# Cutting the last 272 tokens into 144 and 128, with the sums of squares taken inside the last product

## The chip, the cores and the metric

The kernel runs on one core of a Trainium2 chip. The metric is the device time of one execution in microseconds (us), as the median of three runs. The profile is of one execution, and its lines name the core's engines: PE is TensorE (matmuls), PEld its weight loads, DVE is VectorE, ACT is ScalarE, POOL is GpSimd, and SP is the engine whose queue issues the transfers (DMA) to and from memory. Each engine works through its own instructions in the order in which the program wrote them.

## The reference

One layer of a hybrid convolutional decoder on 1024 prompt tokens and 8 x 8 sample tokens, all float32, model width 1024. The part that the change touches is the end: the feed-forward network's down projection, added to x, and the final norm.

```python
h2 = rmsnorm(x, g_ffn)
f = silu(h2 @ w_gate) * (h2 @ w_up)          # width 2816
x = x + f @ w_down
y = rmsnorm(x, g_final)                      # x * rsqrt(mean(x * x) + EPS) * g_final
```

The norm needs, for each token, the sum of the squares of all 1024 channels, so it can start only when every channel of that token has its last addition.

## The kernel before

The tokens lie along the free dimension and the channels along the 128 partitions: `xt` holds x as 8 blocks of 128 channels by T = 1088 tokens. The tokens are two halves of HT = 544, and each half two pieces of CW = 272. Products are made in float16 with both operands split into a high and a low part, so each 128 x 128 weight tile takes three matmuls (high-high, high-low, low-high; `products`, L250, issued at L266).

The down projection runs in four groups of the feed-forward width. The last group (`last_group`, L1636) has four weight tiles per block of channels, so a block of one piece is 12 matmuls. It does the second half of the tokens first, then the first half: block 0 for the whole half, and then, as the list LAST says (L68), blocks 1 to 7 of the first piece (tokens 0 to 271) and blocks 1 to 7 of the last piece (tokens 272 to 543). Each of these is a task (`last_task`, L1578), and the tasks are emitted in this order. A product goes to one of four accumulators in PSUM, used in turn.

After a block's product, VectorE adds it to x (L1554), ScalarE squares the result (L1568), and the square goes into a running sum per half, `squares[hf]`. That addition is GpSimd's (L1575) for the early blocks and VectorE's for one late block (L341, with EPS); the squares of the last one or two blocks are kept apart in `parts` (LAST_PE: one block for an earlier piece, two for the last). An addition of squares is put in the list of late work and emitted at the start of the next task.

The sum over the 128 partitions is a matmul with a matrix of ones, in float32 (`column_sums`, L284; L291 and L297): one such matmul for the running sum and one for each kept square. A float32 matmul is two passes in the profile. For a piece that isn't the last, the sums are put into a later product: `midway` holds pairs of a fraction and a function, and `products` calls the function when that fraction of its matmuls is emitted. SUMS_AT gives 0.8 for a piece of 272, and the call falls into block 3 of the piece that follows. TensorE takes the sums in its own order, so it waits there if a square is not ready. The sums' accumulator is one of two banks called stat.

The final norm (`final_norm`, L1596) then makes 1/sqrt by one activation (L323) and a Newton step of three VectorE instructions (L326 to L328), scales the eight blocks of x (L1626) and writes y (L1629, SP). For a piece that isn't the last this is a stream of steps: one scaling after each later task, so that in the tasks of the last piece VectorE does one addition and one scaling in turn; what is left is emitted after the last task. For the last piece (`fast`) ScalarE and GpSimd do blocks 2 and 5 (L1617, L332, L333, L1624), VectorE the other six, and y is written in four transfers instead of two.

Of the kernel before, what the change touches and what calls it, by code (L numbers as in the profile page):

```python
# [13 lines left out]
D = 1024  # L14
KB = D // P
# [14 lines left out]
HT = T // 2  # L30
CW = 272
# [33 lines left out]


SEVENTHS = "E1 E2 E3 M1 M2 M3 S21 S22 S23 S31 S32 S33 A1 A2 A3"
LAST = [(0, 272), (272, 272)]  # L68


LAST_PE, LAST_POOL = (1, 2), (2, 5)

SUMS_AT = {HT: 0.6, CW: 0.8}

PAIR = [(0, 0), (0, 1), (1, 0), (1, 1)]
TRIPLE = [(0, 0), (0, 1), (1, 0), (1, 1), (2, 0), (2, 1)]
# [65 lines left out]
def trunk(ctx, tc, x, par, sta, stb, w_in, w_o, w_gu, w_ds, w_dl, y, st_out):  # L142
    nc = tc.nc
    pe, act, dve, gps = nc.tensor, nc.scalar, nc.vector, nc.gpsimd
# [15 lines left out]
    def nm(s):  # L160
        cnt[0] += 1
        return f"{s}{cnt[0]}"
# [8 lines left out]
    def small():  # L171
        return sm.tile([P, HT], F32, tag="s", name=nm("s"))
# [10 lines left out]
    def begin(name, turns):  # L183

        cut_banks(part_b, "b", "ps_" + name)
        psum["phase"], psum["turns"], psum["n"] = name, turns, 0
# [6 lines left out]
    def bank2():  # L193
        k = psum["turns"][psum["n"] % len(psum["turns"])]
        psum["n"] += 1
        return psum[k].tile(
            [P, 2, 512], F32, tag="two", name=nm("two"), bufs=psum["turns"].count(k)
        )

    def single():  # L200
        n = 4 if psum["phase"] == "seven" else 2
        return psum["b"].tile([P, 1, 512], F32, tag="one", name=nm("one"), bufs=n)
# [4 lines left out]
    def stat_banks(wide=False):  # L207
        if psum["phase"] == "tail" and wide:
            return bank2()
        if psum["phase"] == "tail":  # L210
            return psum["b"].tile([P, 1, 512], F32, tag="stat", name=nm("stat"), bufs=2)
        if psum["phase"] == "first":
            return psum["b"].tile([P, 1, 512], F32, tag="stat", name=nm("stat"), bufs=2)
        return psum["b"].tile([P, 2, 512], F32, tag="stat", name=nm("stat"))

    def prm(i):
        return par_t[:, i : i + 1]
# [30 lines left out]
    midway = []  # L248

    def products(outs, terms, first=True, last=True, part=(0, None), low_last=None):  # L250


        todo = [(i, q) for i in range(len(terms)) for q in range(3)]
        if low_last:
            todo.sort(key=lambda a: a[1] == low_last)
        one, end = todo[0], todo[-1]
        todo = todo[slice(*part)]
        for n, (i, q) in enumerate(todo):
            for part_, fn in list(midway):
                if n >= int(part_ * len(todo)):  # L260
                    midway.remove((part_, fn))
                    fn()
            w_, col, acts = terms[i]
            wpart, apart = ((0, 0), (0, 1), (1, 0))[q]
            for out, (hl, t0) in zip(outs, acts):
                pe.matmul(  # L266
                    out,
                    w_[:, wpart, col : col + P],
                    hl[:, apart, t0 : t0 + out.shape[1]],
                    start=first and (i, q) == one,  # L270
                    stop=last and (i, q) == end,
                    skip_group_check=not (first and last),
                )
# [26 lines left out]
    def like(ap, t):  # L300

        return t[:, : ap.shape[1]] if len(ap.shape) == 2 else halves(t[:, : 2 * ap.shape[2]])
# [16 lines left out]
    def rstd_kept(sums, inv_n, scale, copied=False):  # L319

        y0 = like(sums, small())
        t = like(sums, small()) if copied else sums
        act.activation(y0, sums, AF.Abs_reciprocal_sqrt, scale=inv_n)  # L323

        def newton():
            dve.scalar_tensor_tensor(t, sums, -0.5 * scale * inv_n, y0, ALU.mult, ALU.mult)  # L326
            dve.tensor_tensor(t, t, y0, ALU.mult)
            dve.scalar_tensor_tensor(sums, t, 1.5 * scale, y0, ALU.add, ALU.mult)  # L328
            if not copied:
                return sums  # L330
            r = like(sums, small())
            act.activation(r, t, AF.Identity, bias=three_halves[:, 0:1])  # L332
            gps.tensor_tensor(r, r, y0, ALU.mult)  # L333
            return sums, r

        return newton
# [11 lines left out]
    ones = cst.tile([P, P], F32, name="ones")  # L348
# [97 lines left out]
    scaled, loaded, sums = set(), {}, {}  # L446
# [60 lines left out]
    def add(ws, emit, post, *bg):  # L507
        tasks.append((ws, emit, post, bg))
# [322 lines left out]
    keep = {}  # L831
# [621 lines left out]
    def last_products(acc, b, t0, cw, ks=None, **kw):  # L1453
        n0, n1 = GROUPS[LASTG]
        w = whl[W_DN[LASTG, f"D{b}"]]
        n = min(cw, CW)
        outs = [acc[:, i, :n] for i in range(cw // n)]
        hf, o = divmod(t0, HT)
        terms = [
            (w, ((k - n0) // 2 + (k - n0) % 2 * 2) * P, [(fl[k, hf], o + i * n) for i in range(cw // n)])  # L1460
            for k in ks or range(n0, n1)
        ]
        products(outs, terms, **kw)
# [80 lines left out]
    def shaped(ap):  # L1544
        return halves(ap) if ap.shape[1] == HT else ap

    def last_post(b, t0, cw):


        def post(acc):  # L1550
            cols = slice(t0, t0 + cw)
            o = shaped(xt[:, b, cols])
            a = acc[:, :, :CW] if cw == HT else acc[:, 0, :cw]
            dve.scalar_tensor_tensor(o, a, IN_SC, o, ALU.mult, ALU.add)  # L1554
            return last_square(b, t0, cw)

        return post

    def last_square(b, t0, cw):
# [8 lines left out]
        act.activation(sq, xt[:, b, cols], AF.Square)  # L1568
        n_pe = LAST_PE[t0 == LAST[-1][0]]
        if b >= KB - n_pe:  # L1570
# [7 lines left out]
    def last_task(b, t0, cw, *bg):  # L1578
        def emit():
            if (b, t0, cw) == (NWIDE - 1, 0, HT):  # L1580
                begin("tail", "aa")
            if (b, t0) == (NWIDE, LAST[0][0]):
                psum["n"] = 2
            if cw == HT or psum["n"] % 4 < 2:
                acc = bank2()
            else:
                acc = single()
                psum["n"] += 1
            last_products(acc, b, t0, cw)
            return acc  # L1590

        add([W_DN[LASTG, f"D{b}"]], emit, last_post(b, t0, cw), *bg)

    squares, parts = {}, {}

    def final_norm(t0, cw, fast):  # L1596

        hf = t0 // HT
        cols = slice(t0, t0 + cw)
        got = []  # L1600

        def sums():
            c = squares[hf][:, t0 - hf * HT : t0 - hf * HT + cw]
            st = column_sums([shaped(p) for p in [c] + parts.pop(t0, [])])
            got.append(rstd_steps(st, 1.0 / D, 1.0) if cw == HT else rstd_kept(st, 1.0 / D, 1.0, fast))

        if fast:
            sums()
        else:
            if cw < HT:  # L1610
                yield
            midway.append((SUMS_AT[cw], sums))
            while not got:
                yield
        if fast:
            for k in LAST_POOL:
                act.activation(xt[:, k, cols], xt[:, k, cols], AF.Copy, scale=prm(PG3 + k))  # L1617
        r = got[0]()
        if fast:
            r, rs = r  # L1620
        for k in range(KB):
            o = shaped(xt[:, k, cols])
            if fast and k in LAST_POOL:
                gps.tensor_tensor(o, o, rs, ALU.mult)  # L1624
            else:
                dve.scalar_tensor_tensor(o, o, prm(PG3 + k), r, ALU.mult, ALU.mult)  # L1626
            n = 2 if fast else 4
            if k % n == n - 1:
                nc.sync.dma_start(  # L1629
                    y[k + 1 - n : k + 1, :, cols].rearrange("k p t -> p k t"),  # L1630
                    xt[:, k + 1 - n : k + 1, cols],
                )
            if k % 2 == 1 or not fast:
                yield

    def last_group():  # L1636
# [23 lines left out]
        for step in SEVENTHS.split():  # L1660
            last_stage(step[:-1], int(step[-1]))
        norms = [Stream(final_norm(HT, HT, False))]
        for b in range(NWIDE):
            last_task(b, 0, HT, lambda: norms[0](1))
        for t0, cw in LAST:
            for b in range(NWIDE, KB):

                def bg(b=b, t0=t0, cw=cw):
                    for st in norms:
                        st(1)  # L1670
                    if b == KB - 1:
                        norms.append(Stream(final_norm(t0, cw, t0 == LAST[-1][0])))
                        if t0 == LAST[-1][0]:
                            for st in norms:
                                st(100)

                last_task(b, t0, cw, bg)
# [93 lines left out]
```

## Time and profile before

| what | us |
|---|---|
| median of three runs | 1006.96 |
| runs | 1006.45, 1006.96, 1006.99 |
| span of the profiled execution | 1006.2 |
| the profiled execution's own time | not given; the page has its span alone |
| VectorE's addition of the last block (L1554) starts | 995.75 |
| first scaling of the last piece (L1626) starts | 999.39 |

Times in the lines are from the start of the span. A line of a timeline has the start, the length, the engine, the line of the program, the operation, what it writes and reads, the shape and the number of instructions that are merged in it; in brackets stands how long the engine was idle before it, and whose result ended that. A line of a group has the number, then the busy time in us, the mean length of one in ns, and the idle time before them. Instructions of one engine overlap a little: the next one starts some 0.08 us before the one ahead of it has ended, unless it needs its result.

### The profile page before, as it was taken

How to read it: one execution, taken by the hardware profiler on the slowest of the kernel's cores; microseconds unless marked ns; L12 is line 12 of the kernel's file. 1: busy time of each engine (PE TensorE's matmuls, PEld its weight loads, DVE VectorE, ACT ScalarE, POOL GpSimd, SP SyncE). 2: the span in 40 equal slices, each digit the busy share in tenths (PEclk: the TensorE clock that was granted, in tenths of full speed). 3: DMA queues.
4: the chain of work that ended last, by engine and by line, in shares of the span. 5: the costliest groups of instructions: out<-in, count | busy, mean ns of one | idle time of the engine just before them, and what ended most of it. 6: DMA issues, size and time to landing. Idle time of an engine off the chain costs nothing.

```text
span 1006.2 us, 19709 instructions
## 1 busy us (share of the span) xinstructions
PE 982.9 (98%) x8466; PEld 828.0 (82%) x8466; DVE 766.0 (76%) x1095; ACT 398.0 (40%) x713; POOL 380.3 (38%) x310
## 2 busy tenths in 40 slices
PE   5999999999999999999999999999999999999996
PEld 4888888888888888888888888888888888888885
DVE  7949999996676778986775767777676678686667
ACT  6612243247362534543322434322243433234433
POOL 3487895656000206222234223223422322273053
PEclk9999999999999999999999999999999999999998
DMA  9020202111500111120112112011211111131104
GB/s 342 40 84 2 67 26 90 43 43 54 208 2 1 43 43 43 43 74 33 64 43 84 43 43 74 33 64 45 83 43 47 70 33 64 64 127 43 42 2 178
DMA packets 17464, 64.60 MB, mean 64 GB/s; under 512 B 1216, under 2 KB 8528, under 8 KB 12512
## 3 DMA queue, kind: packets, MB, share of 16 engines
q1 hardware_dynamic: 17328, 63.25, 18.0%
q8 instruction: 66, 1.08, 0.4%
q14 instruction: 22, 0.18, 0.1%
q0 software_dynamic: 48, 0.09, 0.0%
HBM read 58.28 MB, written 5.05 MB: 63 GB/s over the span
## 4 chain that ended last, share of the span: by engine, by line
PE 72%; DVE 22%; issue 2%; ACT 2%; POOL 0%; DMA 0%; DVEq 0%; ACTq 0%; POOLq 0%
PE two L266 67%; DVE cv L628 11%; PE one L266 4%; DVE u L282 1%; DVE whl L243 1%; DVE xt L1626 1%; DVE h L282 1%; PE stat L291 1%; DVE v L1116 1%; DVE cv L623 1%; DVE xt L1554 0%; DMA xt<-x 0%; DVE u L606 0%; DVE s L770 0%; DVE s L935 0%
## 5 line engine op out<-in xcount | busy, mean ns | idle before, releaser
L266 PEld LDWEIGHTS <-whl 128*128 128x128 f16 x7374 | 721.0, 98 | 136.5 <-issue 2.7
L266 PE MATMUL two<-u,whl 128*128 128x272 f16 x4416 | 523.0, 279 | 0.9 <-DVE s L1324 0.7
L499 POOL TENSOR_TENSOR s<-wf,s 128x512 f32<-128x512 f32 (+1 forms) x32 | 46.9, 1466 | 371.9 <-DVE whl L243 371.9
L266 PE MATMUL two<-v,whl 128*128 128x272 f16 x1536 | 178.7, 279 | 0.5 <-DVE s L935 0.4
L266 PE MATMUL two<-h,whl 128*128 128x272 f16 x1308 | 163.8, 279 | 0.3 <-ACT s L1533 0.3
L242 ACT ACTIVATE whl<-wf 128x512 f16<-128x512 f32 (+1 forms) x150 | 87.6, 589 | 136.6 <-PE two L266 134.6
L628 DVE SCALAR_TENSOR_TENSOR cv<-u,par_t,cv 128x1024 f32<-128x1024 f32 x108 | 130.4, 1291 | 0.1
L243 DVE SCALAR_TENSOR_TENSOR whl<-wf,whl 128x512 f16<-128x512 f32 (+1 forms) x150 | 113.5, 772 | 1.8 <-ACT whl L242 1.8
L1434 DVE SCALAR_TENSOR_TENSOR xt<-two,xt 128x544 f32<-128x544 f32 x108 | 75.8, 721 | 41.4 <-PE two L266 40.9
L488 POOL TENSOR_TENSOR s<-wf 128x512 f32<-128x512 f32 (+1 forms) x32 | 42.3, 1321 | 105.8 <-DVE s L343 91.7
L242 ACT ACTIVATE whl<-s 128x512 f16<-128x512 f32 (+1 forms) x96 | 55.2, 583 | 59.0 <-PE two L266 54.7
L1324 DVE SCALAR_TENSOR_TENSOR s<-two,s 128x544 f32<-128x544 f32 x40 | 28.9, 722 | 57.0 <-PE two L266 56.9
L243 DVE SCALAR_TENSOR_TENSOR whl<-s,whl 128x512 f16<-128x512 f32 (+1 forms) x96 | 66.4, 705 | 0.0
L279 ACT ACTIVATE h<-s 128x544 f16<-128x544 f32 (+1 forms) x60 | 37.1, 626 | 53.2 <-DVE s L1317 43.0
L266 PEld LDWEIGHTS <-u 128*128 128x128 f16 x552 | 49.8, 103 | 9.2 <-issue 1.6
L266 PE MATMUL two<-u,v 128*128 128x272 f16 x480 | 56.3, 279 | 0.0
L266 PEld LDWEIGHTS <-v 128*128 128x128 f16 x480 | 46.9, 98 | 9.1
L266 PE MATMUL one<-v,u 128*128 128x272 f16 (+2 forms) x480 | 49.4, 267 | 0.9 <-DVE v L282 0.4
L1358 DVE SCALAR_TENSOR_TENSOR s<-two,s 128x544 f32<-128x544 f32 x20 | 14.5, 724 | 44.6 <-PE two L266 44.6
L241 POOL TENSOR_TENSOR whl<-wf,whl 128x512 f16<-128x512 f32 x38 | 44.8, 1203 | 2.7 <-ACT whl L240 2.7
L495 POOL TENSOR_TENSOR wf<-wf 128x512 f32<-128x512 f32 (+1 forms) x32 | 45.5, 1423 | 0.0
L282 DVE TENSOR_TENSOR h<-s,h 128x544 f16<-128x544 f32 (+1 forms) x60 | 42.3, 718 | 1.7 <-ACT h L279 0.9
(161 smaller groups left out, 836.7 us busy)
## 6 DMA issues: line engine op xcount, KB each, us to landing
wf<-w_gu SPq DMA_DIRECT2D x22, 1024.0 KB, 4.9
wf<-w_ds SPq DMA_DIRECT2D x12, 768.0 KB, 4.2
wf<-w_in SPq DMA_DIRECT2D x8, 1024.0 KB, 5.1
wf<-w_o SPq DMA_DIRECT2D x6, 1024.0 KB, 4.9
xt<-x SPq DMA_DIRECT2D x3, 1088.0 KB, 11.3
y<-xt SPq DMA_DIRECT2D x2, 1088.0 KB, 4.2
u<-w_in SPq DMA_DIRECT2D x4, 512.0 KB, 7.6
wf<-w_dl SPq DMA_DIRECT2D x2, 1024.0 KB, 4.9
```

The lines of the kernel that those rows point to most:

```text
L241: return whl, lambda: gps.tensor_tensor(lo, wf, hi, ALU.subtract) and None
L242: act.activation(hi, wf, AF.Copy, scale=WSC)
L243: return whl, lambda: dve.scalar_tensor_tensor(lo, wf, WSC, hi, ALU.mult, ALU.subtract) and None
L266: pe.matmul(out, w_[:, wpart, col : col + P], hl[:, apart, t0 : t0 + out.shape[1]], start=first and (i, q) == one, stop=last and (i, q) == ...
L279: act.activation(hi, tmp, AF.Copy)
L282: eng.tensor_tensor(lo, tmp, hi, ALU.subtract)
L488: gps.tensor_tensor(s1, a21, a22, ALU.add)
L495: gps.tensor_tensor(a21, a11, a21, ALU.subtract)
L499: gps.tensor_tensor(src, a12, src, ALU.subtract)
L628: dve.scalar_tensor_tensor(o_, i_, w, c, ALU.mult, ALU.add)
L1324: dve.scalar_tensor_tensor(o, src, IN_SC, other, ALU.mult, ALU.add)
L1434: dve.scalar_tensor_tensor(o, bk[a_][:, :, :CW], IN_SC, o, ALU.mult, ALU.add)
```

## The change

The last piece of 272 tokens becomes two: 144 tokens (272 to 415) and 128 tokens (416 to 543). Each has its own seven products, additions, squares and its own norm; the norm of the 144 is a stream of steps among the tasks of the 128, as that of the first piece is among the tasks of the 144. The sums of the 144 fall into block 3 of the 128.

For the 128 the sum over partitions is no longer made after the last product. A new function, `last_sum`, issues one matmul with the ones: within the last product, before its eighth matmul, for the running sum of blocks 0 to 5, and before its twelfth matmul for the square of block 6. The square of block 7 follows after the product, in `final_norm`.

```diff
-LAST = [(0, 272), (272, 272)]
+LAST = [(0, 272), (272, 144), (416, 128)]
...
-SUMS_AT = {HT: 0.6, CW: 0.8}
+SUMS_AT = {HT: 0.6, CW: 0.8, 144: 0.8}
+
+SUM_EARLY = (0.6, 0.95)
...
+            if (b, t0) == (KB - 1, LAST[-1][0]):
+                midway.append((SUM_EARLY[0], lambda: last_sum(True, False)))
+                midway.append((SUM_EARLY[1], lambda: last_sum(False, False)))
             last_products(acc, b, t0, cw)
...
+    def last_sum(first, last):
+
+        t0, cw = LAST[-1]
+        hf = t0 // HT
+        if first:
+            keep["last sums"] = stat_banks()[:, 0, :cw]
+            p = squares[hf][:, t0 - hf * HT : t0 - hf * HT + cw]
+        else:
+            p = parts[t0].pop(0)
+        pe.matmul(keep["last sums"], ones, p, start=first, stop=last, skip_group_check=True)
...
         if fast:
-            sums()
+            last_sum(False, True)
+            got.append(rstd_kept(keep.pop("last sums"), 1.0 / D, 1.0, True))
```

## The prediction

> **What bounds the kernel now.** I read the page first, then the timeline of VectorE over the last 20 us, then the other engines' lines there, then the groups by shape for 144 and 128 columns.
>
> ```profile
> span 1006.2 us, 19709 instructions
> PE 982.9 (98%) x8466; PEld 828.0 (82%) x8466; DVE 766.0 (76%) x1095; ACT 398.0 (40%) x713; POOL 380.3 (38%) x310
> PE 72%; DVE 22%; issue 2%; ACT 2%; POOL 0%; DMA 0%; DVEq 0%; ACTq 0%; POOLq 0%
> ```
>
> Over the whole span TensorE is the bound, but the change lies in the last 18 us, and there the share says nothing. The timeline of VectorE (start, length, line, shape, and in brackets the idle time before it):
>
> ```profile
> 988.56 0.43 DVE L1554 SCALAR_TENSOR_TENSOR xt<-one,xt 128x272 f32<-128x272 f32 x1
> 988.91 0.77 DVE L1626 SCALAR_TENSOR_TENSOR xt<-xt,par_t,s 128x544 f32<-128x544 f32 x1
> 989.61 0.43 DVE L1554 SCALAR_TENSOR_TENSOR xt<-one,xt 128x272 f32<-128x272 f32 x1
> 990.19 0.44 DVE L1554 SCALAR_TENSOR_TENSOR xt<-two,xt 128x272 f32<-128x272 f32 x1 [0.15 <-PE two L266]
> 990.82 0.45 DVE L326 SCALAR_TENSOR_TENSOR stat<-stat,s 128x272 f32<-128x272 f32 x1 [0.19 <-ACT s L323]
> ...
> 994.58 0.44 DVE L341 SCALAR_TENSOR_TENSOR s<-s,s 128x272 f32<-128x272 f32 x1 [0.30 <-POOL s L1575]
> ...
> 995.75 0.44 DVE L1554 SCALAR_TENSOR_TENSOR xt<-two,xt 128x272 f32<-128x272 f32 x1
> 996.11 1.71 DVE L1626 SCALAR_TENSOR_TENSOR xt<-xt,par_t,stat 128x272 f32<-128x272 f32 x4
> 997.96 0.44 DVE L326 SCALAR_TENSOR_TENSOR s<-stat,s 128x272 f32<-128x272 f32 x1
> ...
> 999.39 2.54 DVE L1626 SCALAR_TENSOR_TENSOR xt<-xt,par_t,stat 128x272 f32<-128x272 f32 x6
> ```
>
> At 988.56 VectorE adds block 1 of the last piece (L1554). From there to the last block's addition at 995.75 its idle times are 0.15, 0.19 and 0.30 us: its queue is nearly full. It does the additions, one scaling (L1626) of the wide norm, then of the first piece's norm the Newton steps (L326 to L328) and four scalings; the other four (996.11) lie under the path from the last addition to the last norm. That path on the other engines, and what leads to the first piece's sums (988.72):
>
> ```profile
> 984.90 2.94 PE L266 MATMUL one<-h,whl 128*128 128x272 f16 x24
> 988.04 0.43 ACT L1568 ACTIVATE s<-xt 128x272 f32<-128x272 f32 x1 [1.13 <-DVE xt L1554]
> 988.72 1.08 PE L297 MATMUL stat<-s,ones 128*128 128x272 f32 x4
> 989.64 1.90 PE L266 MATMUL two<-h,whl 128*128 128x272 f16 x15
> 993.21 0.43 ACT L1568 ACTIVATE s<-xt 128x272 f32<-128x272 f32 x1 [2.06 <-DVE xt L1554]
> 993.78 0.76 POOL L1575 TENSOR_TENSOR s<-s,s 128x272 f32<-128x272 f32 x1 [1.53 <-ACT s L1568]
> 996.28 0.43 ACT L1568 ACTIVATE s<-xt 128x272 f32<-128x272 f32 x1 [0.39 <-DVE xt L1554]
> 996.76 0.73 PE L297 MATMUL stat<-s,ones 128*128 128x272 f32 x2
> 1000.32 2.49 SPq L1629 DMA_DIRECT2D y<-xt  x4
> 1000.40 1.48 POOL L1624 TENSOR_TENSOR xt<-xt,s 128x272 f32<-128x272 f32 x2
> y<-xt SPq DMA_DIRECT2D x2, 544.0 KB, 3.0
> y<-xt SPq DMA_DIRECT2D x4, 272.0 KB, 2.3
> ```
>
> The sum of the last square starts at 996.76, when its square is done (996.28 + 0.43, + 0.05); the two earlier sums are already over, so the early sums take nothing off this path. Hops read here: VectorE's end to ScalarE 0.09, ScalarE to TensorE 0.05, to GpSimd 0.14 (993.64 to 993.78), GpSimd to VectorE 0.03.
>
> I take S, the start of the last L1554, as the hinge: S is 995.75, and 10.45 us follow it to the end of the span.
>
> **Prices of the narrow shapes.** 144 and 128 columns occur at the start of this same kernel:
>
> ```profile
> 9.78 1.90 DVE L770 SCALAR_TENSOR_TENSOR s<-xt,par_t,stat 128x128 f32<-128x128 f32 x7
> 13.52 0.88 DVE L282 TENSOR_TENSOR v<-s,v 128x128 f16<-128x128 f32 x4
> 14.36 0.31 DVE L759 SCALAR_TENSOR_TENSOR u<-u 128x144 f32<-128x144 f32 x1
> 14.59 0.28 DVE L282 TENSOR_TENSOR v<-s,v 128x128 f16<-128x128 f32 x1
> 18.28 1.45 DVE L770 SCALAR_TENSOR_TENSOR s<-xt,par_t,stat 128x144 f32<-128x144 f32 x5
> L759 DVE SCALAR_TENSOR_TENSOR u<-u 128x128 f32<-128x128 f32 x1 | 0.3, 293 | 0.3 <-ACT u L757 0.3
> L279 ACT ACTIVATE v<-s 128x128 f16<-128x128 f32 x8 | 1.8, 302 | 0.0
> L675 POOL TENSOR_TENSOR u<-u 128x128 f32<-128x128 f32 x4 | 1.8, 454 | 0.2
> 22.42 0.83 PE L266 MATMUL one<-v,u 128*128 128x128 f16 x12
> 23.60 4.66 PE L266 MATMUL one<-v,u 128*128 128x144 f16 x72
> 28.61 0.91 PE L266 MATMUL one<-v,u 128*128 128x144 f16 x12
> ```
>
> VectorE, start to start. Scaling with a per-row factor (L770 is L1626's form): 128 columns (1.90 - 0.34) / 6 = 0.26, 144 columns (1.45 - 0.35) / 4 = 0.275, 272 columns (1.71 - 0.49) / 3 = 0.41. Additions: 128 columns (0.88 - 0.28) / 3 = 0.20, 144 columns 0.22 (14.36 to 14.59, less 0.01 for rounding), 272 columns 0.35 (988.56 to 988.91). So half a tile costs 0.6 of a tile. One result is there after 0.29 (128) and 0.31 (144). A Newton step depends on the one before it: its length + 0.03, so 0.48, 0.335 and 0.325. ScalarE's square: 0.30 for 128, some 0.315 for 144. GpSimd's add: 0.45 and some 0.48. The narrow addition reads PSUM, and no row has that at 128 columns: the SBUF rows are one end (0.20), and the wide cost of 0.35 the other; I take 0.20, because at 272 columns L1554 (PSUM) and L341 (SBUF) agree, 0.44 and 0.44.
>
> [...]
>
> TensorE: block by block it fills four accumulators in turn, so it can be four blocks ahead of VectorE's additions and no more. 144 columns (4.66 - 0.91) / 60 = 0.0625 a matmul, 128 columns (0.83 - 0.22) / 11 = 0.056; 272 columns 1.90 less a last length of 0.28, over 14: 0.116. A block of 12 costs 0.75 + 0.67 in place of 1.39: +0.2 us for seven blocks. A pass of a sum takes 0.23 at 272 columns (988.72 to 989.64, four); in proportion 0.12 and 0.107. No row has a narrow pass at full clock; at most it costs the wide one's 0.23, 0.11 more for each of the eight passes ahead of S, and most of these lie under VectorE's queue.
>
> **The tail after S.** Everything has 128 columns. L1554 -0.15, square -0.13, sum -0.24 (two passes, 0.12 each), ScalarE's first activation of the norm -0.13 like the square, three Newton steps -0.45: the scalings start 2.54 after S, in place of 3.64. From there to the last DMA issue 2.98 before (SP's four issues end at 1002.81, each 0.44 to 0.47). After: GpSimd's leg shrinks by 0.3 for each of three steps, VectorE's by 0.15 for each of six, but SP's issues stay: 2.20, so -0.78. The middle piece adds two issues to SP's queue, the second after its last scaling (1002.3 by the queue below), done before the last piece's first at 1004.3. The last transfer: 272 KB lands in 2.3, 544 KB in 3.0, so 128 KB in an estimated 1.93: -0.37. Sum -2.25. The four scalings of the middle piece (4 x 0.275) still hide under the path after S (1.5 us until L326).
>
> **S itself: VectorE's queue.** Up to 988.56 nothing changes: the first piece is the same, and TensorE is ahead. From there VectorE has, before the last L1554:
> - middle piece: 7 additions 1.53, the wide norm's scaling 0.69 (988.91 to 989.61), Newton 1.45, five scalings of the first piece 2.05, L341 0.22;
> - last piece: 6 additions 1.21, three more scalings of the first piece 1.23, Newton for the middle piece 1.01, four of its scalings 1.10, L341 0.20.
>
> Together 10.7 us, where before there were 6.25 (6 x 0.35, 0.69, 1.45, 4 x 0.41, 0.35). The growth of 4.4 has three sources: scalings 5 to 8 of the first piece come out from under the tail (1.64), a whole extra norm comes ahead of S (Newton and four scalings, 2.1), and 13 narrow additions and two L341 take 0.7 more than 6 and one wide.
>
> Its waits, by the hops above:
> - 0.6 before the first L326. TensorE begins block 1 of the middle piece at 984.90 and is at the first piece's sums after 33 matmuls, at 987.0; it waits for the square of the first piece's block 7 (988.47). The sums end at 988.47 + 0.05 + 0.73 = 989.25, but ScalarE makes block 2's square first: L1554 at 988.56 + 0.22 + 0.69 = 989.47, square until 990.19. Before, that square ended at 990.50 (989.61 + 0.43, hop, 0.43) and L326 came 0.32 later; so now 990.51. VectorE is free from 989.91, after block 3's addition. Behind TensorE's wait stand only products for which VectorE is late anyway.
> - 0.1 before the middle piece's L341, for GpSimd. So the last piece's first addition comes at 988.56 + 5.94 + 0.7 = 995.2, and block 4's at 998.34 (3 additions, 3 + 1 scalings, Newton).
> - 0.35 before the last piece's L341: GpSimd's add of block 4 ends 998.34 + 0.29 + 0.09 + 0.30 + 0.14 + 0.45, and 0.03 later is 999.65; VectorE is free at 999.29.
> - 0.85 before S. The middle piece's block 7 is added at 994.6 (995.2 less an addition and a scaling), its square is there 0.71 later, and TensorE has that piece's sums done by 995.8. It does three blocks of 0.67 and seven matmuls until 998.3. There, at its eighth matmul, it waits for the running sum from L341 (done 999.95). Then it needs block 6's square: L1554 at 999.855 + 0.29 + 0.09 + 0.30 + 0.05, a weight load of some 0.11, two passes 0.21, the twelfth matmul 0.22, 0.04 to VectorE: 1001.17. VectorE has done one scaling meanwhile and is free at 1000.33. Behind that wait stands the twelfth matmul, and with it S: here the early sum puts a new stall on the path.
>
> S = 988.56 + 10.7 + 1.9 = 1001.17, +5.42. The same ledger for before, 6.25 and waits of 0.94 (the three idle times, with the overlap of 0.08 each, and 0.06), gives 995.75, as seen.
>
> **Sum:** +5.42 - 2.25 = +3.17; span 1009.4. The page gives a span and no time of its own for that execution; the median of the runs lies 0.76 above the span, and I keep that: 1010.1 us.
>
> **Rivals.**
> 1. The stall of the early sums is not on the path, as if all sums came after the last product: S at 1000.33, +2.3, 1009.3. For it: VectorE is free then. Against it: the product's last matmul is queued behind the sum.
> 2. VectorE gets through much faster, by 1.2 us or more (GpSimd's adds earlier, the 0.6 wait gone): about +1.5, 1008.5. Against it: the prices are rows of the same operations.
> 3. Faster: VectorE keeps up, and TensorE sets S. Then S moves by the split 0.2, the middle piece's sums 0.48 and the early sums 0.43, to 996.9, and the tail's 2.25 wins: -1.1, 1005.8. It decides only if 34 instructions on VectorE fit into 8.3 us, with some 0.07 less for each, that is, if a narrow one had no fixed cost at all; the rows show 0.20 for 128 columns.
> 4. The clock drops while TensorE waits from 998.3 to 1000.1. The last matmul of before ended at 997.5, and the granted clock is half from 1000.0 on, 2.5 us later:
>
> ```profile
> 1000.00:1006.20 6.20, 0.00 (x0) 0.50 0.58 197
> ```
>
> The wait is 1.8 us, shorter. At half clock the remaining matmuls and sums take 1.0 more: 1011.1. [...]
> 5. Narrow additions from PSUM lie nearer the wide one's 0.35: a third of the way, 0.05 for each of 13, gives 1010.8; all the way, 0.14, gives 1011.9.
>
> **How the numbers follow.** About 0.2%, 2 us, is what a measurement tells from no change, so slower begins at 1009.0. Chances: forecast 0.62, rival 1 0.16, rival 2 0.07, rival 3 0.04, rival 4 0.06, rival 5 0.05. Faster is rival 3: 0.04. Same is rival 2, a third of rival 1 and 0.05 of the forecast's lower edge: 0.17. Slower is the rest, 0.79. The range, 1008.4 to 1011.5, holds all but rival 3 and the edges of 2, 4 and 5.
>
> **What would show it.** In the profile after: the last L1554 near 1001; TensorE idle for over 1 us inside the last product, released by L341; L1626 of 272 columns among the last piece's additions; VectorE hardly idle from 990.5 to 999.3; about 8.2 us from S to the end. It is wrong if S lies before 999, or if TensorE runs the last product without a wait.

## The result

The changed kernel takes 1010.39 us (median of five runs, 1009.7 to 1010.61), the kernel before 1006.96: a ratio of 1.0032, with a 95% interval of 1.0021 to 1.0043. It is 3.4 us slower. The forecast was 1010.1, range 1008.4 to 1011.5.

The profile after, first the page. The lines of `final_norm` now stand at L1643 and the last block's addition at L1556 (before L1626 and L1554); the other helpers moved by two.

```profile
span 1008.6 us, 19930 instructions
PE 984.1 (98%) x8554; PEld 830.5 (82%) x8554; DVE 768.6 (76%) x1114; ACT 399.1 (40%) x721; POOL 381.3 (38%) x315
```

The shares tell nothing of it, as forecast. The timeline of VectorE after, from block 1 of the middle piece on:

```profile
988.08 0.29 DVE L1556 SCALAR_TENSOR_TENSOR xt<-one,xt 128x144 f32<-128x144 f32 x1
...
989.96 0.45 DVE L328 SCALAR_TENSOR_TENSOR stat<-stat,s 128x272 f32<-128x272 f32 x1 [0.46 <-ACT s L325]
...
993.89 0.31 DVE L343 SCALAR_TENSOR_TENSOR s<-s,s 128x144 f32<-128x144 f32 x1
...
994.74 0.28 DVE L1556 SCALAR_TENSOR_TENSOR xt<-two,xt 128x128 f32<-128x128 f32 x1
994.94 0.49 DVE L1643 SCALAR_TENSOR_TENSOR xt<-xt,par_t,stat 128x272 f32<-128x272 f32 x1
...
996.56 0.31 DVE L328 SCALAR_TENSOR_TENSOR stat<-stat,s 128x144 f32<-128x144 f32 x1
...
997.89 0.28 DVE L1556 SCALAR_TENSOR_TENSOR xt<-two,xt 128x128 f32<-128x128 f32 x1
...
999.20 0.29 DVE L343 SCALAR_TENSOR_TENSOR s<-s,s 128x128 f32<-128x128 f32 x1 [0.29 <-POOL s L1577]
...
999.61 0.35 DVE L1643 SCALAR_TENSOR_TENSOR xt<-xt,par_t,stat 128x144 f32<-128x144 f32 x1
1000.73 0.29 DVE L1556 SCALAR_TENSOR_TENSOR xt<-one,xt 128x128 f32<-128x128 f32 x1 [0.77 <-PE one L268]
1000.94 1.18 DVE L1643 SCALAR_TENSOR_TENSOR xt<-xt,par_t,stat 128x144 f32<-128x144 f32 x4
1002.32 0.29 DVE L328 SCALAR_TENSOR_TENSOR s<-stat,s 128x128 f32<-128x128 f32 x1 [0.20 <-ACT s L325]
...
1003.30 1.64 DVE L1643 SCALAR_TENSOR_TENSOR xt<-xt,par_t,stat 128x128 f32<-128x128 f32 x6
```

The last addition, S, is at 1000.73. Scalings of the first piece (272 columns, 994.94) now stand between the last piece's additions, then a whole norm's Newton steps (996.56) and scalings of 144 columns. Between 990 and 998.9 VectorE shows no wait of its own but for 0.1 at 993.8; then it waits 0.29 for GpSimd's sum and 0.77 for TensorE. TensorE in the last product:

```profile
996.75 1.22 PE L268 MATMUL one<-h,whl 128*128 128x128 f16 x19
999.55 0.49 PE L1610 MATMUL stat<-s,ones 128*128 128x128 f32 x2 [1.58 <-DVE s L343]
999.88 0.39 PE L268 MATMUL one<-h,whl 128*128 128x128 f16 x4
1000.15 0.49 PE L1610 MATMUL stat<-s,ones 128*128 128x128 f32 x2
1000.48 0.22 PE L268 MATMUL one<-h,whl 128*128 128x128 f16 x1
1001.48 0.49 PE L1610 MATMUL stat<-s,ones 128*128 128x128 f32 x2 [0.79 <-ACT s L1570]
```

After 19 matmuls (block 6 and seven of block 7) it stands for 1.58 us, released by L343, which is L341 of before; then four matmuls, the second early sum, and the twelfth matmul. After the product it still waits 0.79 for block 7's square: the tail gained nothing from the early sums.

**A common zero.** The eleven kept traces (of programs that are the same up to there) differ by up to 1.3 us in when they reach one and the same instruction of the last group: the late addition of squares of the first piece (L341 or L343) starts at 987.17 before and at 985.83 in e2. Between before and after the gap is 0.32 near VectorE's 60th instruction (L282 at 31.91, L284 at 31.59) and 0.50 at block 0 of the last group. So I compare the traces from the addition of block 0 of the whole half, which the change does not touch; before:

```profile
973.54 0.72 DVE L1554 SCALAR_TENSOR_TENSOR xt<-two,xt 128x544 f32<-128x544 f32 x1 [2.34 <-PE two L266]
```

and after:

```profile
973.04 0.72 DVE L1556 SCALAR_TENSOR_TENSOR xt<-two,xt 128x544 f32<-128x544 f32 x1 [2.34 <-PE two L268]
```

From it to S are 22.21 us before (995.75 - 973.54) and 27.69 after: +5.48. From S to the end of the span are 10.46 before and 7.84 after: -2.62. The trace's net is +2.86; the medians differ by 3.43, with an interval of 2.1 to 4.3.

### The profile page after: what moved, and what is told of

Its sections match the earlier page's. It is cut to its first block, busy times and chain, and to the rows that moved or that the text cites. A ratio compares the mean times of both kernels' runs of the same rounds, so it can differ in the third digit from the quotient of the medians.

```text
span 1008.6 us, 19930 instructions
## 1 busy us (share of the span) xinstructions
PE 984.1 (98%) x8554; PEld 830.5 (82%) x8554; DVE 768.6 (76%) x1114; ACT 399.1 (40%) x721; POOL 381.3 (38%) x315
## 4 chain that ended last, share of the span: by engine, by line
PE 72%; DVE 23%; issue 2%; ACT 2%; POOL 0%; DMA 0%; DVEq 0%; ACTq 0%; POOLq 0%
PE two L268 67%; DVE cv L630 12%; PE one L268 4%; DVE xt L1643 1%; DVE u L284 1%; DVE whl L245 1%; DVE h L284 1%; PE stat L293 1%; DVE v L1118 1%; DVE xt L1556 1%; DVE cv L625 1%; DMA xt<-x 0%; DVE s L772 0%; DVE u L608 0%; DVE s L937 0%
## 5 line engine op out<-in xcount | busy, mean ns | idle before, releaser
L268 PE MATMUL two<-h,whl 128*128 128x272 f16 (+2 forms) x1344 | 164.2, 276 | 0.5 <-ACT s L1535 0.3
L284 DVE TENSOR_TENSOR h<-s,h 128x544 f16<-128x544 f32 (+1 forms) x60 | 42.2, 718 | 1.7 <-ACT h L281 0.9
```

What stands on the lines that cost most here:

```text
L268: pe.matmul(out, w_[:, wpart, col : col + P], hl[:, apart, t0 : t0 + out.shape[1]], start=first and (i, q) == one, stop=last and (i, q) == ...
L284: eng.tensor_tensor(lo, tmp, hi, ALU.subtract)
```

## The experiments

Each was run beside the kernel before on the same chip (medians there 1007.09 to 1007.16). "S" is the last addition, counted from block 0's addition, as a difference from the kernel before; "tail" is the rest of the span, likewise; "sum" is both, from the traces' full digits.

| kernel | S | tail | sum | median us | ratio to before, 95% |
|---|---|---|---|---|---|
| the change | +5.48 | -2.62 | +2.86 | 1010.39 | 1.0021 to 1.0043 |
| e1, late sums | +4.63 | -2.63 | +2.00 | 1009.03 | 1.0010 to 1.0027 |
| e2, two pieces, early sums | +1.12 | +0.01 | +1.13 | 1008.03 | 1.0002 to 1.0019 |
| e3, the change without four scalings | +4.73 | -2.67 | +2.06 | 1009.60 | 1.0014 to 1.0033 |
| e4, before without four scalings | 0.00 | +0.01 | +0.01 | 1007.05 | 0.9990 to 1.0007 |
| e5, two pieces, 400 and 144 | +2.78 | -1.18 | +1.59 | 1008.87 | 1.0007 to 1.0025 |
| e6, two pieces, 304 and 240 | +0.41 | -0.38 | +0.02 | 1007.25 | 0.9993 to 1.0011 |
| e7, e1 without the middle norm | +3.02 | -2.48 | +0.53 | 1007.54 | 0.9997 to 1.0015 |
| e8, e7 without four scalings | +3.02 | -2.67 | +0.35 | 1007.56 | 0.9992 to 1.0009 |
| e9, e8 without the middle sums | +2.34 | -2.62 | -0.28 | 1008.68 | 1.0004 to 1.0023 |

### e1: the split without the early sums

The kernel before, with the list of pieces alone changed.

```diff
-LAST = [(0, 272), (272, 272)]
+LAST = [(0, 272), (272, 144), (416, 128)]
-SUMS_AT = {HT: 0.6, CW: 0.8}
+SUMS_AT = {HT: 0.6, CW: 0.8, 144: 0.8}
```

> Three pieces as in the change, but all sums of the last piece come after its last product, as in the kernel before. Queue theory (VectorE's queue sets the end and the early sums add a stall on the path): no wait of TensorE inside the last product, so the last addition starts some 0.84 us earlier than in the changed kernel, 11.8 us after block 1 of the middle piece's addition instead of 12.65; the tail is unchanged; about 1009.5 us. Rival (the early sums lie beside VectorE's work and cost nothing): no change against the changed kernel, 1010.4. Rival (they are a gain, since two sums are taken off the tail): 0.4 us more, 1010.8.

VectorE's end of the queue in e1:

```profile
998.68 0.29 DVE L341 SCALAR_TENSOR_TENSOR s<-s,s 128x128 f32<-128x128 f32 x1 [0.29 <-POOL s L1575]
998.89 0.28 DVE L1554 SCALAR_TENSOR_TENSOR xt<-one,xt 128x128 f32<-128x128 f32 x1
999.09 0.35 DVE L1626 SCALAR_TENSOR_TENSOR xt<-xt,par_t,stat 128x144 f32<-128x144 f32 x1
999.36 0.28 DVE L1554 SCALAR_TENSOR_TENSOR xt<-one,xt 128x128 f32<-128x128 f32 x1
```

and TensorE's:

```profile
996.22 1.50 PE L266 MATMUL one<-h,whl 128*128 128x128 f16 x24
999.03 1.56 PE L297 MATMUL stat<-s,ones 128*128 128x128 f32 x6 [1.30 <-DVE s L341]
```

The last addition follows the scaling ahead of it without a wait, 11.80 us after block 1 of the middle piece (987.56), where the change has 12.65: the stall cost 0.85. TensorE had the last product done at 997.7 and stood idle for VectorE. The medians say 1.4 between the two kernels, with intervals that overlap; I take the size from the trace.

### e2: the early sums without the split

The changed kernel, with the pieces of before.

```diff
-LAST = [(0, 272), (272, 144), (416, 128)]
+LAST = [(0, 272), (272, 272)]
```

> The last piece stays 272 wide, only the early sums inside its last product are added. Queue theory: block 6's square is ready 0.5 us after TensorE reaches the twelfth matmul, then two passes of 0.23 and a load of 0.1; the last addition starts 1.1 to 1.2 us later than in the kernel before and nothing comes back in the tail, since the last square is what the tail waits for: about 1008.1 us. Rival (early sums are a gain or nothing): 1006.5 to 1007.0.

VectorE in e2, then TensorE, with ScalarE's square of block 6:

```profile
995.53 0.44 DVE L1556 SCALAR_TENSOR_TENSOR xt<-two,xt 128x272 f32<-128x272 f32 x1 [1.10 <-PE two L268]
```

```profile
993.73 0.73 PE L1610 MATMUL stat<-s,ones 128*128 128x272 f32 x2
...
994.12 0.43 ACT L1570 ACTIVATE s<-xt 128x272 f32<-128x272 f32 x1 [1.06 <-DVE xt L1556]
994.30 0.63 PE L268 MATMUL two<-h,whl 128*128 128x272 f16 x4
...
994.76 0.62 PE L1610 MATMUL stat<-s,ones 128*128 128x272 f32 x2
995.22 0.28 PE L268 MATMUL two<-h,whl 128*128 128x272 f16 x1
996.55 0.72 PE L1610 MATMUL stat<-s,ones 128*128 128x272 f32 x2 [1.05 <-ACT s L1570]
```

and the last product of the kernel before:

```profile
994.16 1.55 PE L266 MATMUL two<-h,whl 128*128 128x272 f16 x12
```

S comes 1.12 us later, and the tail is the same to 0.01: TensorE waits 1.05 us for block 7's square all the same. The size is as I expected, the way is not. Block 6's square is ready at 994.55, before TensorE comes to it at 994.76, so there is no wait for it. The passes of the sums themselves take the time, 0.57 (993.73 to 994.30) and 0.46 (994.76 to 995.22); some 0.1 is the wait for L343 ahead of them. In the kernel before the last product ends at 995.71, only 0.04 ahead of S, so there is no room for them. The early sums alone cost 1.1 us in the trace; the medians say 0.9, and the interval only just excludes no change.

### e3 and e4: four scalings left out, in the change and in the kernel before

Both leave out VectorE's scalings of blocks 4 to 7 of the first piece; those blocks of y stay without their norm.

```diff
-            else:
+            elif (t0, cw) != (0, CW) or k < 4:
                 dve.scalar_tensor_tensor(o, o, prm(PG3 + k), r, ALU.mult, ALU.mult)
```

> The changed kernel, with the scalings of blocks 4 to 7 of the first piece left out (so these blocks of y are not normalised for the first 272 tokens); transfers stay. Queue theory: 1.64 us of VectorE's work in front of the last addition is gone; half of it turns into waits for squares and sums, so the last addition starts 0.8 us (at most 1.6) earlier: about 1009.6 us. Rival (TensorE's narrower matmuls and sums set the end): no change, 1010.4.

> The kernel before, with the same four scalings left out (blocks 4 to 7 of the first 272 tokens are not normalised). Queue theory: in the kernel before they lie under the path from the last addition to the last norm, so the last addition and the tail stay where they are: 1007.0 us, within 0.2. Rival (VectorE's total work counts wherever it lies): 1.6 us less, 1005.3.

The same 1.64 us of work is worth 0.75 us in the change (S +4.73 for +5.48) and nothing in the kernel before (S to 0.01). Where it went, in e3:

```profile
995.55 0.29 DVE L1556 SCALAR_TENSOR_TENSOR xt<-one,xt 128x128 f32<-128x128 f32 x1 [0.79 <-PE one L268]
```

and in e4:

```profile
994.44 0.44 DVE L1554 SCALAR_TENSOR_TENSOR xt<-two,xt 128x272 f32<-128x272 f32 x1
996.65 0.44 DVE L326 SCALAR_TENSOR_TENSOR s<-stat,s 128x272 f32<-128x272 f32 x1 [1.77 <-ACT s L323]
```

In e4 VectorE waits 1.77 us where the scalings were: they lay under the path of the last square and sum. In e3 the freed time turns half into a wait of 0.79 for block 3's product, in which TensorE takes the middle piece's sums.

### e5 and e6: two pieces, cut elsewhere

```diff
-LAST = [(0, 272), (272, 272)]
+LAST = [(0, 400), (400, 144)]
-SUMS_AT = {HT: 0.6, CW: 0.8}
+SUMS_AT = {HT: 0.6, 400: 0.8}
-        n = min(cw, CW)
+        n = CW if cw == HT else cw
```

e6 has 304 and 240 instead.

> Two pieces as in the kernel before, cut at 400 instead of 272, sums after the last product: the last piece has 144 columns, nearly as narrow as in the change, but there is no third piece and no extra norm. Queue theory: the tail after the last addition is some 2.1 to 2.4 us shorter, as in the change; the first piece's norm is wider (Newton steps of 0.61, scalings of 0.54) and must fit into the last piece's 5 us, so the last addition starts 2.0 to 2.3 us later (not 5.4) and the scalings left after it are too long to hide by 0.7: about 1008.0 us, 1 over the kernel before. Rival (the narrow last piece itself is what costs, by its many small instructions): 1010 or more. Rival (only the extra piece costs): the tail's gain stays whole, 1004.7.

> Two pieces cut at 304. Queue theory: VectorE just keeps up, the last addition starts where it did, the tail is 0.4 us shorter: 1006.6 us, hardly to be told from the kernel before. Rival (VectorE has no room left in the kernel before): the last addition moves by 0.5 us or more and the time is 1007.1 or over.

VectorE in e5:

```profile
991.96 0.31 DVE L1554 SCALAR_TENSOR_TENSOR xt<-two,xt 128x144 f32<-128x144 f32 x1 [1.15 <-PE two L266]
...
997.26 0.30 DVE L1554 SCALAR_TENSOR_TENSOR xt<-two,xt 128x144 f32<-128x144 f32 x1
997.47 2.24 DVE L1626 SCALAR_TENSOR_TENSOR xt<-xt,par_t,stat 128x400 f32<-128x400 f32 x4
999.64 0.30 DVE L326 SCALAR_TENSOR_TENSOR s<-stat,s 128x144 f32<-128x144 f32 x1
```

e5 loses 2.78 us at S, half of what the change loses, and gets 1.18 back: the four wide scalings fill 997.47 to 999.71, so L326 comes 2.38 after S, where the change has 1.59 (1002.32 - 1000.73), which is 0.8 of the 1.4 us that its tail gains less. S moved 0.5 to 0.8 more than I expected, and the time is 0.9 over what I expected. The first line shows a wait that I had not counted: VectorE waits 1.15 for block 3's product, in which TensorE takes the first piece's sums (0.15 in the kernel before). So neither rival holds: the narrow last piece is not what costs (1010 or more), and two pieces don't keep the whole gain (1004.7). e6 is the same as the kernel before: S loses 0.41, where I expected nothing, and the tail gives 0.38. Its rival, that VectorE has no room left in the kernel before, comes nearer: S moved almost the 0.5 it asks for.

### e7, e8, e9: taking VectorE's extra work away from e1

e7 is e1 with the Newton steps and scalings of the middle piece left out (its 144 tokens of y stay without a norm). e8 leaves out the four scalings of e3 besides, and e9 the middle piece's sums and their activation as well.

```diff
-        r = got[0]()
+        r = got[0]() if t0 != 272 else None
...
-            else:
+            elif t0 != 272:
                 dve.scalar_tensor_tensor(o, o, prm(PG3 + k), r, ALU.mult, ALU.mult)
```

> Three pieces with all sums of the last piece after its last product, and the middle piece's Newton steps and scalings left out (its 144 tokens of y are not normalised; the sums and the activation stay). Against the run with late sums this takes 2.1 us of VectorE's work from in front of the last addition. Queue theory with its waits: some 0.5 of it turns into waits, the last addition starts 10.2 us after block 1 of the middle piece (11.8 with late sums alone, 7.2 before), about 1007.5 us. Rival (work alone counts): 9.7 us, 1006.9. Rival (TensorE's sums and narrow products set the end): no change, 1009.0.

> As the run without the middle norm, and the scalings of blocks 4 to 7 of the first piece are left out too. Queue theory with its waits: nothing more is gained, since TensorE waits in block 3 of the last piece for the middle piece's sums (its last squares come late, behind the first norm's Newton steps and GpSimd's adds), and four and a half narrow blocks follow; the last addition stays at 10.2 us, 1007.5 us. Rival (work alone counts): 1.6 us less, 1005.9.

> As the run without the middle norm and without four scalings, and the middle piece's sums in block 3 of the last piece are left out too (its 144 tokens of y stay without a norm), so TensorE has nothing to wait for there. If that wait is what holds the last addition once VectorE's extra work is gone, the last addition starts 0.6 us earlier, 9.6 us after block 1 of the middle piece (10.2 with the sums, 7.2 before): then the chain of squares, GpSimd's adds and L341 is next; some 1006.9 us. Rival (the wait is harmless): no change, 1007.5.

e7's S is 10.20 us after block 1 of the middle piece, as expected: 1.61 less than e1 for 2.1 us of work. e8's is the same 10.20, though it does another 1.64 us less. VectorE in e8 now waits for TensorE, block after block:

```profile
995.73 0.29 DVE L1554 SCALAR_TENSOR_TENSOR xt<-one,xt 128x128 f32<-128x128 f32 x1 [0.79 <-PE one L266]
996.39 0.29 DVE L1554 SCALAR_TENSOR_TENSOR xt<-two,xt 128x128 f32<-128x128 f32 x1 [0.38 <-PE two L266]
...
997.80 0.29 DVE L341 SCALAR_TENSOR_TENSOR s<-s,s 128x128 f32<-128x128 f32 x1 [0.44 <-ACT s L1568]
```

TensorE's weight loads for the middle piece's sums wait in their turn, first for the running sum, then for the kept square:

```profile
994.38 0.30 PEld L297 LDWEIGHTS stat<-s,ones 128*128 128x128 f32 x2 [0.24 <-DVE s L341]
995.01 0.30 PEld L297 LDWEIGHTS stat<-s,ones 128*128 128x128 f32 x2 [0.33 <-ACT s L1568]
```

In e9, without those sums, VectorE waits for GpSimd:

```profile
997.03 0.29 DVE L341 SCALAR_TENSOR_TENSOR s<-s,s 128x128 f32<-128x128 f32 x1 [0.90 <-POOL s L1575]
```

By the trace S moves 0.68 in e9, to 9.55 after block 1 (0.6 expected). Its runs scatter from 1006.6 to 1009.4, its median is 1.1 above that of e8 (run on another chip), and its interval lies above the kernel before; its profiled execution took 1007.04. So the time does not bear the trace out here, and I don't know why the other runs of e9 are longer. That the wait for the middle sums was next is shown by the trace alone.

Even with all of this left out, S is 2.3 us later than in the kernel before. No run pointed to a version that beats it: the split can give 2.6 at the tail, and e9, which leaves the middle piece without a norm, still pays nearly all of it ahead of S.

## Why the prediction was right

**Prices of the narrow shapes: right.** An addition of 128 columns from PSUM starts 0.20 before the next instruction (994.74 to 994.94), as taken. Rival 5 falls. Per column the narrow addition is still the dearer one: 0.20 us for 128 columns, 0.35 for 272 (988.56 to 988.91 before).

**S: right, term by term.** From block 1 of the middle piece, forecast and measured:

| step | forecast | measured |
|---|---|---|
| first L326 | 1.95 | 1.88 |
| L341 of the middle piece | 5.81 | 5.81 |
| block 4 of the last piece | 9.78 | 9.81 |
| L341 of the last piece | 11.09 | 11.12 |
| S | 12.61 | 12.65 |

S came at +5.48 for a forecast of +5.42. The sources are shown to different degrees. That scalings 5 to 8 of the first piece came out from under the tail: e3 and e4, by the pair. That an extra norm stands ahead of S: e7, 1.61 of its 2.1. The 0.7 for the narrow additions has no run of its own; only their prices are shown. The new stall: e1, 0.85 for 0.85. e2 shows the cost of sums in front of a product without the split, but there it is their own time, not a wait for an operand. Rival 1 falls with e1.

**What the ledger did not say.** Work and waits are not two independent columns. Taking 1.64 us of work away gives 0.75 (e3), and after 2.1 the next 1.64 give nothing (e8): by the traces, behind VectorE's queue stands TensorE's wait for the middle piece's sums, behind that GpSimd's adds. Rival 3, that TensorE sets S at 996.9 once VectorE keeps up, was therefore mis-built: with VectorE relieved S is still 3.0 us late (e8), not 0.7 (its 1.1 less the 0.43 for the early sums, which e8 does not have). The middle piece's sums are 0.68 of that (e9). The other 2.3 no run takes apart; the trace of e9 has VectorE's 0.90 for GpSimd's adds among them. So VectorE's longer queue, with the new stall, is why S loses 5.5 and not 3.0; but even without them the split gains nothing: e8's interval holds 1.

**The tail: one term mis-sized.** Forecast -2.25, measured -2.62. From S to the first scaling 2.57 (2.54 forecast), from there to the last DMA issue 2.19 (2.20), but from the last issue to the end 3.07, where before had 3.84: -0.77 for the -0.37 forecast. I had the landing of the transfers nearly right (1.93 for 1.9; the last of the four took 1.99):

```profile
y<-xt SPq DMA_DIRECT2D x4, 128.0 KB, 1.9
```

but took the group's median of 2.3 for the last transfer of before. That one landed 2.62 us after its issue, the three ahead of it 2.19 to 2.32 after theirs. So 0.63 of the 0.77 lie in the landing of the last transfer.

**Around the span: wrong.** I kept 0.76 us, the median of the runs less the span of the profile. In the runs of the changed kernel, each with its own span, the difference is 1.7 to 1.9 (1010.43 for 1008.6), and two later runs of the kernel before with a span of 1006.2 took 1007.94 and 1008.03. So the profiled execution of before took an estimated 1008.0, one us over its median; its trace is the latest of the eleven at block 0. The forecast of the span, 1009.4, was 0.8 too high (0.49 for that late start, 0.37 for the tail, less 0.06 at S), and that error and this one nearly cancel. By the trace the change costs 2.86 us; the agreement of 1010.1 with 1010.39 is in part luck, that of the steps is not.

**The clock: right in what came of it, not in the reason.** TensorE's clock was granted in full (1.00) through the wait of 1.58 us:

```profile
998.00:1001.00 3.00, 1.15 (x9) 0.84 (x9) 1.95 (x9) 0.93 (x3) 0.46 (x1) 1.00 0.42 147
1001.00:1002.50 1.50, 0.49 (x2) 0.30 (x2) 1.30 (x6) 0.80 (x4) 0.00 (x0) 1.00 0.60 183
1002.50:1003.00 0.50, 0.00 (x0) 0.00 (x0) 0.43 (x3) 0.36 (x2) 0.00 (x0) 0.54 0.00 0
```

(A row has the stretch and its length, the busy time and instructions of PE, PEld, DVE, ACT and POOL, then the granted clock, the DMA share and GB/s.) It fell to half at 1002.54, 0.57 us after the last matmul's end (1001.97), not 2.5 as in the kernel before. So 2.5 us is no fixed delay, and that this wait passed at full clock is in part luck: that it would, because it is shorter than 2.5, was my estimate, and no run shows what sets the delay. Something near rival 4 came in e5: TensorE waits 1.72 us there, and the clock falls at 997.14, half a microsecond after the wait and within the last sums:

```profile
996.64 2.23 PE L297 MATMUL stat<-s,ones 128*128 128x144 f32 x6 [1.72 <-DVE s L341]
993.73:997.14 3.41, 1.69 (x22) 1.30 (x18) 3.37 (x9) 0.89 (x3) 0.48 (x1) 1.00 0.20 77
997.15:999.00 1.85, 1.60 (x5) 1.01 (x4) 1.85 (x5) 0.42 (x3) 0.00 (x0) 0.50 0.39 148
```

By the trace it cost e5 nothing: VectorE goes from its four scalings to L326 without a wait.

## What to carry to other kernels

When a tail is cut narrower, everything that belonged to the piece cut off moves ahead of the last addition: its norm, and the work that the old tail was hiding. Count that on the engine whose queue is full there, instruction by instruction with its start-to-start time, before counting the tail's gain. And a sum put into a product early is only early if its operands are ready there: TensorE took it in the program's order, and it held up the product behind it, by its own passes at the least (0.57 and 0.46 us in e2) and by a wait of 1.58 us in the change. It took nothing off a path that waits for a later operand (the tail of e2 is the same to 0.01).

## What the runs showed of the hardware

- Executions of programs that are the same up to the late addition of the first piece (L341, L343 in e2) reach it up to 1.3 us apart (987.17 before, 985.83 in e2). Of the 0.50 us between before and after, 0.32 are there near the 60th of VectorE's 1,100 instructions (31.91 and 31.59). A total of 1007 us hides 1 us of change behind that; the trace, counted from an untouched instruction, resolves far less (e4 gives S and tail to 0.01).
- The granted clock did not fall a fixed time after the last matmul: 0.57 us after it in the change (1001.97 to 1002.54), 2.48 in the kernel before (997.49 to 999.97), an estimated 0.8 in e1 (its clock is 0.95 on average from 996 to 1002, and the last matmul ends at 1000.59), and 1.73 before its end in e5 (997.14 and 998.87). Nor did it go by the length of the wait alone: it fell 0.5 us after a wait of 1.72 us in e5, and stayed at 1.00 through one of 1.58 in the change and for 2.48 without a matmul in the kernel before. What sets the time of the fall, no run shows.
